# Two results to x's staging buffer and four more C slots in a matmul of undone prefix sums

## The chip, the cores and the metric

The kernel runs on 1 core of one Trainium2 chip. The metric is the device time of one execution in microseconds; lower is better. Before the change the median of three runs is 1509.22 us (1507.74 to 1509.64).

## The reference

```python
B, S, D = 8, 2048, 2048          # x: [8, 2048, 2048] float32, w: [2048, 2048] float32
cs = np.cumsum(x, axis=1)
diff = cs - (cs moved down by one row, zeros first)   # which is x again
return np.matmul(diff, w)        # float32
```

The difference of neighbouring prefix sums is x, so the kernel computes x @ w: a matrix of 16384 x 2048 by one of 2048 x 2048.

## The kernel before, in words

The rows of x are cut into 128 row tiles of 128 rows (`P = 128`, `END = 128`). The kernel has three parts.

**Plain part (row tiles 0 to 3, `PLAIN = 4`).** While w arrives, these tiles are multiplied as bf16. The sums stand in the eight banks of TensorE's accumulator memory, first for the left half of the columns (h = 0), then for the right (h = 1). `plain_out` copies finished banks of 128 x 512 to buffers on ScalarE (ACT) and notes them in `done`, and `put` stores them later: the first round from GpSimd's queue, the second, with one left-over product of tile 3, from SyncE's (SP). The buffers are two halves of `F[:, 2]` for tile 0 in the first round; a `wb` buffer of the pool `ring` for tile 0 in the second; and a buffer `o` of the pool `opool`, which has five, for all others. In the first round five results take an `o`. In the second it is six, and `left_over` takes a seventh. A buffer that is asked for again is free when its last store has landed.

`F` has five places of 128 x 1024 f32 in which the halves of later tiles of x are staged; `where` says which: tiles 4 and 6 use `F[:, 0]`, `F[:, 3]` and `F[:, 1]`, `F[:, 4]`, tile 7 `F[:, 2]` and `F[:, 3]`, tile 5 part of `xP`, in which the four plain tiles stood.

**First group of four row tiles (`group_plain`, tiles 4 to 7).** The rest is done in f16 with a seven-product (Strassen-like) scheme over 2 x 2 blocks. x is loaded (`load`), weighed for its scale (`weigh` on ACT, `scale_of` on VectorE, DVE), narrowed to f16 in place (`narrow`, ACT) and transposed by DMA from SP (`turn`). In the group `g` is tile 4, `h` tile 6, `g + 1` tile 5, `h + 1` tile 7. `product` (line 516) multiplies into a pair of banks called X, Y, Z or V; `keeps` (line 543, ACT) copies a pair of banks, scaled, to a pair of C slots; `adds` (line 546, DVE) adds a pair of banks to it; `puts` (line 557, SP) stores the pair and gives the slots back. `total` (line 506, DVE) makes sums of blocks of x such as S1, `block` (lines 357 and 361) narrows w's blocks, and `less` (line 499, DVE) makes differences of them. All x DMAs and the stores share SP's queue, in program order.

The order of the keeps in `group_plain` is C11g, C11h, C22 (of g + 1), C12g, C12h, C22 (of h + 1), C21 (g + 1), C21 (h + 1). Each takes two slots from the front of the list `free`; `put` appends a slot at the end when its store is issued in the program.

**Later groups (`group`, tiles 8 to 127, 30 groups).** The same scheme with one more level for some of the products (`quarter`, line 535).

What sets the order: each engine's instructions are chained in program order by `after`; the framework places tiles in memory, and makes the first user of a tile wait until the last users of whatever stood in that memory are done. The pools of the plain part (`ring`, `o`, `first` with `xP`) are closed before `C` and `inner` are opened, so these lie where those lay: the 7 slots of C where the ring's buffers lay, `inner` (24 pieces of 128 x 512 f16) where the `o` buffers and most of `xP` lay. `inner` holds sums of x (pieces 0 to 7) and differences of w (pieces 8 to 23; pieces 16 to 23 are written by `in_3.first()`, near the end of `group_plain`).

Of the kernel before, what the change touches and what calls it, by code (L numbers as in the profile page):

```python
# [10 lines left out]
def kernel(  # L11
# [18 lines left out]
    f32 = mybir.dt.float32  # L30
# [11 lines left out]
    PLAIN = 4  # L42
# [33 lines left out]
    def after(engine, ask):  # L76
        if engine in last:
            with tc.issue_after(last[engine].ins):
                said = ask()
        else:  # L80
            said = ask()
        last[engine] = said[-1] if isinstance(said, tuple) else said
        return said
# [77 lines left out]
    with tc.tile_pool(name="ring", bufs=7) as ring, tc.tile_pool(  # L161
# [81 lines left out]
        def here(h, r):  # L243
            return range(1 if h == 0 and r == PLAIN - 1 else 2)
# [14 lines left out]
        def put(c, rows, columns, queue=nc.gpsimd):  # L259
            return queue.dma_start(out2[rows, columns], c)  # L260

        def plain_out(h, r):
            for n in here(h, r):
                if h == r == 0:
                    c = F[:, 2, ds(n * NB, NB)]
                elif h == 0 or r > 0:
                    c = opool.tile([P, NB], f32, name="o")
                else:
                    c = ring.tile([P, NH], bf16, name="wb").bitcast(f32)
                after("act", lambda: nc.scalar.copy(c, ps[r][n]))  # L270
                done.append((c, ds(r * P, P), ds(h * NH + n * NB, NB)))
# [22 lines left out]
        for ko in range(KO - KQ):  # L294
# [9 lines left out]
            if ko in turns:  # L304
                q, a = turns[ko]
# [15 lines left out]
        for r in range(PLAIN):  # L321
            for ko in range(KO - KQ, KO):
                plain(0, r, ko)
            plain_out(0, r)
# [22 lines left out]
        with tc.issue_after(whole_max.ins):  # L347
            for c, rows, columns in done:
                put(c, rows, columns)
# [15 lines left out]
        def finish_row(r):  # L365
            for ko in range(KO - KQ, KO):
                plain(1, r, ko)
            plain_out(1, r)
# [45 lines left out]
        for c, rows, columns in done:  # L414
            after("sp", lambda: put(c, rows, columns, nc.sync))
# [34 lines left out]
    inner = inpool.tile([P, 24, NB], f16, name="inner")  # L450
# [6 lines left out]
    S1 = [Part(inner[:, ds(2 * i, 2), :]) for i in range(2)]  # L457
    passing = [Quarter(inner[:, j, :]) for j in range(4, 8)]
    free = [cpool.tile([P, NB], f32, name=f"c{i}") for i in range(7)]

    def pair():
        return [one_c() for _ in range(2)]
# [92 lines left out]

    def put(c, t, at):
        after("sp", lambda: nc.sync.dma_start(out2[ds(t * P, P), ds(at * NB, NB)], c))
        free.append(c)

    store = put  # L560

    def puts(c, t, h):
        for n in range(2):
            put(c[n], t, 2 * h + n)
# [446 lines left out]
```

## Time and profile before

| | |
|---|---|
| Time, median of 3 runs (lowest, highest) | 1509.22 us (1507.74, 1509.64) |
| Span of the profiled execution, first to last instruction | 1507.4 us |
| Its own time beside the span | not shown on the page |
| DVE, ACT busy | 88%, 61% of the span |
| DMA traffic | 354 MB, 235 GB/s mean |
| Plain part, `group_plain`, later groups on TensorE | about 0 to 76, 76 to 134, 134 to 1507 us |

The profile names engines PE (TensorE's matmuls), PEld (its weight loads), DVE, ACT, POOL (GpSimd) and SP. A row of a timeline has start, duration, engine, line, operation, output and inputs, and how many equal instructions were merged; in brackets stands the idle time of the engine before it and what ended it. A row of the waits has the total in us, how often, and the longest. A row of DMA issues has the queue, the count, the KB of each and the median us from issue to landing.

### The profile page before, as it was taken

Reading aid. Unit: us, or ns where it says so; the run is one execution under the profiler, and the core shown is the slowest. Engines: PE = TensorE matmul, PEld = TensorE weight load, DVE = VectorE, ACT = ScalarE, POOL = GpSimd, SP = SyncE. Lnnn points to the kernel's source line nnn. Section 1 sums busy time; section 2 is a strip of 40 time slices with the busy share of each in tenths; the row PEclk is TensorE's granted clock in tenths of the full one; section 3 lists DMA queues with packets and bytes.
Section 4 is the critical chain, followed back from the end, with each engine's and each line's share of the span. In section 5 each row is a group of like instructions: output and inputs, shape, how many; then the busy total and the mean of one; then the engine's idle time right before and its main releaser. Section 6 shows DMA issues by size and latency. Waiting matters only on the chain.

```text
span 1507.4 us, 21215 instructions
## 1 busy us (share of the span) xinstructions
PE 1480.5 (98%) x6799; PEld 661.8 (44%) x6799; DVE 1329.6 (88%) x2419; ACT 914.2 (61%) x1301; POOL 328.9 (22%) x360
## 2 busy tenths in 40 slices
PE   8988999999999999999999999999999999999998
PEld 3433444444444444444444444444444444444443
DVE  7987778889998899998899998999898899888997
ACT  5865656656656656656656656556656556666552
POOL 0100001122221122222122222122222122212222
PEclk9999999999999999999999999999999999999999
DMA  9988979988888988788987888987788988888962
GB/s 359 354 216 243 248 228 249 254 243 211 232 223 229 253 242 212 235 221 233 252 244 205 235 220 240 249 245 205 233 217 244 256 224 219 233 219 241 253 177 105
DMA packets 378912, 354.28 MB, mean 235 GB/s; under 512 B 274928, under 2 KB 275440, under 8 KB 378672
## 3 DMA queue, kind: packets, MB, share of 16 engines
q1 hardware_dynamic: 378240, 351.09, 83.5%
q0 software_dynamic: 560, 1.84, 0.3%
q8 instruction: 53, 0.87, 0.2%
q14 instruction: 59, 0.48, 0.1%
HBM read 151.52 MB, written 136.31 MB: 191 GB/s over the span
## 4 chain that ended last, share of the span: by engine, by line
PE 75%; DVE 13%; issue 4%; DMA 4%; ACT 3%; SPq 0%; DVEq 0%; ACTq 0%
PE b L535 37%; PE b L516 36%; DVE c L546 9%; DVE inner L506 3%; DMA W<-in_w_dram 2%; PE b L250 2%; ACT c L543 1%; DMA x<-F 1%; DVE W L499 1%; DMA W<-in_x_dram 0%; DMA out_dram<-c 0%; DVE x L506 0%; ACT W L361 0%; ACT waste L112 0%; DVE m L129 0%
## 5 line engine op out<-in xcount | busy, mean ns | idle before, releaser
L546 DVE SCALAR_TENSOR_TENSOR c<-b,u,c 128x512 f32<-128x512 f32 x1048 | 736.6, 745 | 125.4 <-PE b L535 81.3
L516 PE MATMUL b<-W,x 128*128 128x512 f16 x3072 | 717.9, 380 | 5.9 <-ACT c L543 3.8
L543 ACT ACTIVATE c<-b,u 128x512 f32<-128x512 f32 x496 | 315.5, 680 | 283.6 <-issue 147.8
L516 PEld LDWEIGHTS <-x 128*128 128x128 f16 x3072 | 300.9, 98 | 370.5 <-issue 8.4
L143 ACT ACTIVATE F<-F,s 128x1024 f16<-128x1024 f32 x246 | 282.4, 1148 | 162.3 <-DVE s L131 158.3
L535 PE MATMUL b<-W,inner 128*128 128x512 f16 x1392 | 338.3, 379 | 0.0
L112 ACT ACTIVATE waste<-F 128x1024 uint8<-128x1024 f32 x246 | 259.5, 1055 | 115.0 <-DMA F<-in_x_dram 110.9
L535 PEld LDWEIGHTS <-inner 128*128 128x128 f16 x1744 | 168.5, 98 | 215.3 <-DVE c L546 15.3
L132 POOL TENSOR_SCALAR u<-m,uw 128x1 f32<-128x1 f32 x124 | 66.6, 542 | 817.0 <-DVE m L129 809.0
L535 PEld LDWEIGHTS <-x 128*128 128x128 f16 x1560 | 152.1, 98 | 195.9 <-issue 14.6
L535 PE MATMUL b<-W,x 128*128 128x512 f16 x968 | 234.2, 379 | 1.5
L503 POOL TENSOR_TENSOR flow<-W 128x512 f16<-128x512 f16 x140 | 163.6, 1195 | 291.2 <-PE b L535 286.8
L506 DVE TENSOR_TENSOR x<-x,x 128x1024 f16<-128x1024 f16 (+1 forms) x214 | 147.2, 700 | 6.2 <-PE b L516 1.1
L503 POOL TENSOR_TENSOR flow<-W,W 128x512 f16<-128x512 f16 x84 | 94.9, 1160 | 0.0
L535 PE MATMUL b<-flow,x 128*128 128x512 f16 x352 | 90.3, 379 | 2.5 <-DVE c L546 2.5
L506 DVE TENSOR_TENSOR inner<-x,x 128x1024 f16<-128x1024 f16 (+1 forms) x122 | 67.4, 553 | 3.3 <-DMA x<-F 3.3
L250 PE MATMUL b<-wb,xP 128*128 128x512 bf16 x240 | 57.4, 393 | 5.0 <-ACT wb L234 3.6
L535 PE MATMUL b<-inner,x 128*128 128x512 f16 x240 | 61.6, 379 | 0.7 <-DVE x L506 0.7
L535 PE MATMUL b<-inner 128*128 128x512 f16 x240 | 61.6, 379 | 0.4 <-DVE c L546 0.4
L506 DVE TENSOR_TENSOR inner<-x,inner 128x512 f16<-128x512 f16 x60 | 51.7, 862 | 0.0
L112 ACT ACTIVATION_READ_ACCUMULATOR waste<-F 128x1 f32 x246 | 46.6, 190 | 0.0
L506 DVE TENSOR_TENSOR x<-inner,x 128x1024 f16<-128x1024 f16 x62 | 42.4, 683 | 3.2
(56 smaller groups left out, 510.2 us busy)
## 6 DMA issues: line engine op xcount, KB each, us to landing
out_dram<-c SPq DMA_DIRECT2D x496, 256.0 KB, 3.2
F<-in_x_dram SPq DMA_DIRECT2D x246, 512.0 KB, 4.9
W<-in_w_dram SPq DMA_DIRECT2D x32, 512.0 KB, 9.6
W<-in_x_dram SPq DMA_DIRECT2D x16, 256.0 KB, 7.7
x<-F SPq DMA_TRANSPOSE x246, 3.4
out_dram<-o SPq DMA_DIRECT2D x7, 256.0 KB, 3.6
spill<-flow SPq DMA_DIRECT2D x3, 512.0 KB, 2.6
out_dram<-o POOLq DMA_DIRECT2D x5, 256.0 KB, 4.2
```

The lines of the kernel that those rows point to most:

```text
L112: lambda: nc.scalar.activation(waste, where[t][i], ABS, scale=1.0 / ROW, accum_out=sums_of[t][:, i : i + 1],),
L132: after("pool", lambda: nc.gpsimd.tensor_scalar(u, m, uw, None, MUL))
L143: lambda: nc.scalar.activation(narrowed(t)[:, ds(i * NH, NH)], where[t][i], COPY, scale=s),
L250: lambda: nc.tensor.matmul(ps[r][n], xP[:, r, ko, :], wb[h, ko][:, ds(n * NB, NB)], start=(ko == 0), stop=(ko == KO - 1),),
L499: after("dve", lambda: nc.vector.tensor_tensor(dst[k], p[k], q[k], SUB))
L503: after("pool", lambda: nc.gpsimd.tensor_tensor(passed[k], i.t21[k], i.Q2[k], SUB))
L506: after("dve", lambda: nc.vector.tensor_tensor(dst.all, p.all, q.all, op))
L516: said = nc.tensor.matmul(to[n], a[k], b[k][:, n, :], start=(first and k == 0), stop=(k == KH - 1), skip_group_check=True,)
L535: said = nc.tensor.matmul(to, a[k], b[k], start=(first and k == 0), stop=(k == 3), skip_group_check=True)
L543: after("act", lambda: nc.scalar.activation(c, p, COPY, scale=u))
L546: after("dve", lambda: nc.vector.scalar_tensor_tensor(c, p, u, c, MUL, ADD))
```

## The change

In the second round the two results of plain row tile 3 go to the halves of `F[:, 2]`, as those of tile 0 do in the first round. Four more slots for C, called `extra`, are cut out of `inner`: pieces 16 and 17, 18 and 19, 20 and 21, 22 and 23, each read as 128 x 512 f32. They stand at the front of `free`, so the first four keeps take them, and `put` doesn't give them back. All engines issue the same operations in the same order as before; only buffers and waits differ.

```diff
         def plain_out(h, r):
             for n in here(h, r):
-                if h == r == 0:
+                if (h, r) in ((0, 0), (1, PLAIN - 1)):
                     c = F[:, 2, ds(n * NB, NB)]
                 elif h == 0 or r > 0:
                     c = opool.tile([P, NB], f32, name="o")
...
     free = [cpool.tile([P, NB], f32, name=f"c{i}") for i in range(7)]
+    extra = [inner[:, ds(j, 2), :].rearrange("p a c -> p (a c)").bitcast(f32) for j in range(16, 24, 2)]
+    free = extra + free
...
     def put(c, t, at):
         after("sp", lambda: nc.sync.dma_start(out2[ds(t * P, P), ds(at * NB, NB)], c))
-        free.append(c)
+        if not any(c is e for e in extra):
+            free.append(c)
```

## The prediction, made before the changed kernel ran

> **What bounds the kernel now.** I read the page's head first, then who waited for whom, then TensorE's timeline at the waits that the change touches, and last the queues behind these waits.
>
> ```profile
> span 1507.4 us, 21215 instructions
> PE 1480.5 (98%) x6799; PEld 661.8 (44%) x6799; DVE 1329.6 (88%) x2419; ACT 914.2 (61%) x1301; POOL 328.9 (22%) x360
> ```
>
> PE is the bound: 1480.5 of 1507.4 us. An edit pays only where it removes idle time of PE, and only if nothing takes it back before the steady groups begin. The waits on stores, and PE's own waits, are these:
>
> ```profile
> ACT c L543 <- DMA out_dram<-c: 8.7, 3, 5.8
> ACT o L270 <- DMA out_dram<-o: 5.8, 1, 5.8
> PE b L516 <- ACT c L543: 3.8, 2, 3.4
> PE b L516 <- DVE inner L506: 2.3, 1, 2.3
> PE b L516 <- ACT o L270: 1.7, 1, 1.7
> ```
>
> ACT waits once for 5.8 us until an o buffer is stored, and once for 5.8 us until a C buffer is. PE's timeline (start, duration, what, idle before it) has the price of both:
>
> ```profile
> 75.70 4.05 PE L516 MATMUL b<-W,x 128*128 128x512 f16 x18
> 81.41 10.09 PE L516 MATMUL b<-W,x 128*128 128x512 f16 x46 [1.66 <-ACT o L270]
> 93.77 3.61 PE L516 MATMUL b<-W,inner 128*128 128x512 f16 x16 [2.27 <-DVE inner L506]
> ...
> 101.29 10.67 PE L516 MATMUL b<-W,x 128*128 128x512 f16 x48 [0.44 <-ACT c L543]
> ...
> 115.25 0.38 PE L516 MATMUL b<-W,x 128*128 128x512 f16 x1
> 119.01 11.34 PE L516 MATMUL b<-W,x 128*128 128x512 f16 x44 [3.38 <-ACT c L543]
> ```
>
> Together 1.66 + 2.27 + 0.44 + 3.38 = 7.75 us. The last gap costs more than itself, as two windows show (us, PE busy and count, granted clock, DMA share, GB/s):
>
> ```profile
> 92.00:96.00 4.00, 2.23 (x11) 1.00 0.90 260
> 119.01:124.00 4.99, 4.99 (x16) 0.66 0.50 197
> ```
>
> A full PE starts a matmul every 0.216 us: the row at 81.41 has 46 in 10.09 us, of which the last takes 0.38, so (10.09 - 0.38) / 45. In the 4.99 us after the 3.38 us gap 23 would fit; the granted clock is 0.66 and there are 16, so 7 x 0.216 = 1.5 us more. After the 2.27 us gap the clock stayed at 1.00. What the edits can touch is thus 7.75 + 1.5 = 9.3 us, 0.6% of the span.
>
> **Part 1: two results of row tile 3 go to F.** Their copies were the sixth and seventh users (with the left-over product's) of five o buffers; now only five are asked for in that round. No instruction is added: two copies and two stores keep their places and sizes and change their buffer. ACT's queue around them:
>
> ```profile
> 73.45 1.54 ACT L270 COPY o<-b 128x512 f32<-128x512 f32 x3
> 80.78 0.59 ACT L270 COPY o<-b 128x512 f32<-128x512 f32 x1 [5.78 <-DMA out_dram<-o]
> 81.97 0.69 ACT L384 ACTIVATE o<-b,uw 128x512 f32<-128x512 f32 x1 [0.61 <-DMA out_dram<-o]
> ...
> 85.36 2.33 ACT L143 ACTIVATE xP<-xP,s 128x1024 f16<-128x1024 f32 x2 [0.48 <-DVE s L131]
> 87.60 3.21 ACT L361 ACTIVATE W<-W,uinv 128x1024 f16<-128x1024 f32 x3
> 90.72 1.24 ACT L543 ACTIVATE c<-b,u 128x512 f32<-128x512 f32 x2
> ```
>
> The fourth copy would start at 74.9 and end at 75.5; the left-over product is done when PE turns to the next line at 75.70, so its copy runs at 75.95, 6.0 us earlier than 81.97. Behind it tile 5 is weighed and narrowed. Is its data there? SP's timeline has the load's issue, the view of DMAs its size and time to landing, DVE's timeline the work ahead of the scale:
>
> ```profile
> 68.99 0.33 SPq L404 DMA_DIRECT2D xP<-in_x_dram  x1
> xP<-in_x_dram SPq DMA_DIRECT2D x1, 1024.0 KB, 5.3
> 70.72 8.02 DVE L357 TENSOR_SCALAR W<-W,uinv 128x1024 f16<-128x1024 f32 x12
> ```
>
> It landed at 68.99 + 5.3 = 74.3. From the left-over copy to the narrowing it takes 85.36 - 81.97 = 3.4 us, the last 0.5 of them for DVE's scale, and DVE is free of its blocks at 78.74. So narrowing tile 5 moves by the full 6.0 us, from 85.36 to 79.35, and B22's three blocks end at 84.8 instead of 90.8. PE's gap of 1.66 goes: bank 7 is free at 75.5.
>
> The cost of F: tile 7's first load goes to the same part of F and now waits for those two stores. They are issued on SP at about 79.8 and 80.3 and land some 4 us later (rows below), so at 84.3; SP reaches that load after tile 5's transposes, at 83.9. Cost 0.4 us on a load that starts 4.8 us earlier than before: nothing, as ACT weighs tile 7 only after the B22 blocks.
>
> **Part 2: four more C slots.** C11g and C11h, the first four results, take them, are never put back, and the seven old slots begin with C22g. No instruction moves. What changes is who waits for which store. Going through the list by hand: before, C12h[1] took the slot of C11h[0], whose store is the first of the six at 111.80; now C12h takes slots that were never used. C22h[1] took a slot long free; now it takes that of C12g[0], whose store is the third of the same six. So the wait doesn't vanish, it moves one step down and to a store 1.2 us later:
>
> ```profile
> 111.78 0.69 ACT L543 ACTIVATE c<-b,u 128x512 f32<-128x512 f32 x1 [3.47 <-PE b L516]
> 118.27 0.69 ACT L543 ACTIVATE c<-b,u 128x512 f32<-128x512 f32 x1 [5.80 <-DMA out_dram<-c]
> ...
> 122.22 2.32 ACT L143 ACTIVATE F<-F,s 128x1024 f16<-128x1024 f32 x2
> ```
>
> SP's timeline has that store's issue, and the view of DMAs its KB and us to landing:
>
> ```profile
> 112.95 0.47 SPq L557 DMA_DIRECT2D out_dram<-c  x1
> out_dram<-c SPq DMA_DIRECT2D x1, 256.0 KB, 6.5
> ```
>
> The third store lands at 112.95 + 6.5 = 119.45 by the old clock of events. ACT can then keep C22h[1] until 120.15 and go on to narrow tile 10, which stood at 122.22: 2.05 us saved on ACT. On PE, the product into Y starts at 115.25 at once and ends 16 x 0.216 = 3.45 us later, at 118.7; the next product's second matmul needs Z's second bank, free at 120.2. A gap of 1.3 us takes the place of the 3.5 us from matmul to matmul (119.01 - 115.25, less one spacing) and of 1.5 us of slow clock: PE saves 3.7 us, if the clock holds as it did after 2.27.
>
> **The wait that part 2 adds.** The extra slots lie in the tile named inner, which was first written by DVE's sum S1. Now ACT writes it first, with C11g[0], and so it is ACT that waits until that memory's last users are done: the o stores, and both transposes that read tile 5 out of xP (the changed program lists these semaphores at that instruction). Behind it in ACT's queue stand three B22 blocks, tile 7's weighing, and all later keeps. When does this wait end? In SP's timeline and the view of DMAs (KB, us to landing) stand the last o stores, one of them alone, and the two transposes, the second alone:
>
> ```profile
> 76.18 6.84 SPq L260 DMA_DIRECT2D out_dram<-o  x7
> 79.82 0.47 SPq L260 DMA_DIRECT2D out_dram<-o  x1
> out_dram<-o SPq DMA_DIRECT2D x1, 256.0 KB, 3.9
> 86.53 2.62 SPq L156 DMA_TRANSPOSE x<-xP  x2
> 87.87 1.29 SPq L156 DMA_TRANSPOSE x<-xP  x1
> x<-xP SPq DMA_TRANSPOSE x1, 3.3
> ```
>
> The store at 79.82 is the fifth of the seven; two more at its pace of 0.5 us free SP at 81.3 (before, they waited for ACT until 83.0). The transposes follow: the second starts at 81.3 + 1.34 = 82.65 and lands 3.3 later, at 85.95, if the engines are free; behind stores that land until about 85 it may be 87.1. I take 86.3, nearer the bare row. ACT is ready at 84.8, so it waits 1.5 us, and C11g's keep moves from 90.72 to 86.4: of the 6.0 us, 4.3 are left. Below: 85.0 (no wait, gain 5.7). Above: 87.1 (gain 3.6). The old S1 waited for the same transposes on DVE, at no cost.
>
> **The sum.** Up to 101 us: PE's work without gaps from 75.70 would reach the S1 product (93.77) after 18 + 46 matmuls, at 89.5; S1 follows C11g's keep and releases PE 4.3 us earlier, at 89.5 too. So 4.2 us is saved there. ACT, now 4.3 earlier, leaves most of the gap at 101.29. PE at 115: 4.3 earlier. Part 2: PE another 3.7 (8.0 in all), but ACT, and with it DVE's scales, its adds and SP's queue, only another 2.05, so 6.4 in all. What is late next is where these meet, in the timelines of DVE, PE and SP and in a window (busy time and count of PE, PEld, DVE, ACT and POOL, clock, DMA share, GB/s):
>
> ```profile
> 149.31 0.69 DVE L506 TENSOR_TENSOR inner<-x,x 128x1024 f16<-128x1024 f16 x1 [1.11 <-DMA x<-F]
> 152.35 1.02 PE L535 MATMUL b<-flow,x 128*128 128x512 f16 x4 [1.78 <-DVE c L546]
> 159.21 1.04 PE L535 MATMUL b<-inner,x 128*128 128x512 f16 x4 [0.66 <-DVE x L506]
> 140.46 6.83 SPq L156 DMA_TRANSPOSE x<-F  x2
> 132.00:166.00 34.00, 31.07 (x142) 13.46 (x141) 25.47 (x58) 21.61 (x33) 2.17 (x3) 1.00 1.05 249
> ```
>
> In the next group DVE's S1h waits for tile 11's transposes, PE for an add behind it. These transposes stand on SP behind stores of C22h and C12h, so they come 6.4 earlier, not 8.0. PE, up to 1.6 us ahead of them, waits up to 3.4 us instead of 1.78, and from 152 on all is 6.4 us earlier. Later groups have nearly no idle PE and no wait that the change touches. So the span becomes 1507.4 - 6.4 = 1501.0. The page shows no time but the span; the median of the runs is 1509.2, 1.8 above it, and I carry that over: 1502.8.
>
> [...]
>
> **Rivals.**
> *Half clock at the new gap.* The gap of up to 3.4 us at 152 lies between 2.27 (no drop) and 3.38 (drop). If the clock falls, PE loses 1.5 us again, of which the 0.66 us gap at 159.21, set by DVE and ACT, hides about half: 1502.8 + 0.9 = 1503.7. [...] Chance 0.2.
> *The store and the transposes come sooner.* With ACT's wait at 84.8 gone and the third store no later than PE, all 9.3 us are saved, if tile 11 also keeps up: 1499.9. For it: the wait has only 1.5 us to lose. Against: six stores land late as a block. Chance 0.13.
> *Tile 11's transposes do not move as much.* Two of them held SP for 6.83 us at 140.46, against 2.62 at 86.53: 4.2 us of queue, in a stretch with a DMA share of 1.05. If this hold grows by as much, because transfers now crowd into a full queue, 2.2 us are left: 1507.0. Against: the lull before it (a share of 0.50 from 119 to 124) takes in what comes earlier. Chance 0.12.
> *It doesn't do what it says.* If the new wait ends only where the old keep stood (90.7) and PE's slow stage is kept by the moved store wait, nothing is won: 1509. Chance 0.04.
> *Slower.* The slots go round in another order for the 30 later groups. If one keep in each waited for its store, the gain is gone at 6.4 / 30 = 0.21 us a group, and at 0.35 us the time is 1502.8 + 10.5 = 1513.3. Against: the first row of the waits has three such waits in the whole run, and seven slots still go round first in, first out. Chance 0.04.
>
> **How the numbers follow.** The forecast has 0.47. Range: from the second rival's 1499.9 to the third's 1507.0; this leaves out the last two and the edges. A measurement of this kernel can tell 0.2%, 3.0 us: faster is below 1506.2. That holds the forecast, the first two rivals and a quarter of the third: 0.83; three quarters of the third and most of the fourth are the same: 0.12; the last and the rest are slower: 0.05.
>
> **What would show it.** Right: no ACT wait on a store at the copies to o or F; C11g's keep near 86.4 after a wait for the transposes x<-xP of about 1.5 us; PE without gaps from 75.7 to about 96; a wait on a store at C22h[1] instead of C12h[1], PE's gap there about 1.3 us and the clock at 1.00; S1h in the next group near 142.9. Wrong: tile 5's transposes landing after 88, PE's gap at C22h over 2.5 us, S1h later than 146, or waits of c on stores that recur in every group.

## The result, and the profile after

The changed kernel takes 1502.92 us (median of 5 runs, 1500.95 to 1503.45) against 1508.17 us for the kernel before (5 runs, 1507.74 to 1509.64). The ratio is 0.9961, 95% interval 0.9949 to 0.9974: 3.9 to 7.7 us faster, 5.3 by the medians. In a second comparison it took 1502.34 us, ratio 0.996 (0.9946 to 0.9973). The profiled execution has a span of 1500.3 us, 7.1 less than the one before (of the runs of before, the profiled one is among the longer, of the changed kernel among the shorter).

The waits after (total us, times, longest), those that answer to the rows shown of before:

```profile
ACT c L545 <- DMA out_dram<-c: 6.3, 4, 2.5
ACT inner L545 <- DMA x<-xP: 3.2, 1, 3.2
PE b L518 <- DMA F<-in_x_dram: 1.4, 1, 1.4
PE b L518 <- ACT c L545: 0.8, 3, 0.4
```

No copy to an o buffer or to F waits for a store any more. The wait on a C store is 2.5 us at its longest instead of 5.8, and a wait of 3.2 us for the transposes that read xP is new. PE's timeline:

```profile
75.51 13.98 PE L518 MATMUL b<-W,x 128*128 128x512 f16 x64
90.85 3.61 PE L518 MATMUL b<-W,inner 128*128 128x512 f16 x16 [1.36 <-DMA F<-in_x_dram]
94.30 3.63 PE L518 MATMUL b<-W,x 128*128 128x512 f16 x16
98.38 0.38 PE L518 MATMUL b<-W,x 128*128 128x512 f16 x1 [0.44 <-ACT c L545]
98.95 10.30 PE L518 MATMUL b<-W,x 128*128 128x512 f16 x47 [0.20 <-ACT c L545]
...
116.57 17.21 PE L518 MATMUL b<-W,x 128*128 128x512 f16 x79 [0.19 <-ACT c L545]
...
145.12 1.02 PE L537 MATMUL b<-flow,x 128*128 128x512 f16 x4 [1.88 <-DVE c L548]
```

The 64 matmuls from 75.51 now run in one piece. The gap ahead of the S1 product shrank from 2.27 to 1.36 us (the view names a load; what came last is S1 on DVE, in the next block, which ends at 90.50: PE starts 0.35 us behind it). The gap of 3.38 us is 0.19. ACT, DVE and SP at the same places:

```profile
75.71 0.69 ACT L384 ACTIVATE o<-b,uw 128x512 f32<-128x512 f32 x1 [0.42 <-PE b L375]
79.10 2.33 ACT L143 ACTIVATE xP<-xP,s 128x1024 f16<-128x1024 f32 x2 [0.48 <-DVE s L131]
81.34 3.22 ACT L361 ACTIVATE W<-W,uinv 128x1024 f16<-128x1024 f32 x3
87.78 1.26 ACT L545 ACTIVATE inner<-b,u 128x512 f32<-128x512 f32 x2 [3.22 <-DMA x<-xP]
...
115.83 0.69 ACT L545 ACTIVATE c<-b,u 128x512 f32<-128x512 f32 x1 [2.55 <-DMA out_dram<-c]
116.41 2.32 ACT L143 ACTIVATE F<-F,s 128x1024 f16<-128x1024 f32 x2
89.82 0.68 DVE L508 TENSOR_TENSOR inner<-x,x 128x1024 f16<-128x1024 f16 x1
142.08 0.69 DVE L508 TENSOR_TENSOR inner<-x,x 128x1024 f16<-128x1024 f16 x1 [1.20 <-DMA x<-F]
82.10 2.94 SPq L156 DMA_TRANSPOSE x<-xP  x2
...
133.80 2.06 SPq L559 DMA_DIRECT2D out_dram<-c  x2
135.96 4.14 SPq L156 DMA_TRANSPOSE x<-F  x2
```

And the clock, in the windows behind the two gaps (us, PE busy and count, granted clock, DMA share, GB/s):

```profile
116.57:120.00 3.43, 3.43 (x16) 1.00 0.39 142
145.12:149.00 3.88, 3.88 (x18) 1.00 0.95 297
```

### The profile page after: what moved, and what is told of

Read it like the earlier page. It is cut to its first block, busy times and chain, and to the rows that moved or that the text cites. A ratio compares the mean times of both kernels' runs of the same rounds, so it can differ in the third digit from the quotient of the medians.

```text
span 1500.3 us, 21209 instructions
## 1 busy us (share of the span) xinstructions
PE 1477.7 (98%) x6793; PEld 660.9 (44%) x6799; DVE 1329.1 (89%) x2419; ACT 914.2 (61%) x1301; POOL 329.0 (22%) x360
## 4 chain that ended last, share of the span: by engine, by line
PE 74%; DVE 13%; issue 4%; DMA 4%; ACT 3%; SPq 0%; DVEq 0%; ACTq 0%
PE b L537 37%; PE b L518 35%; DVE c L548 9%; DVE inner L508 3%; PE b L250 2%; DMA W<-in_w_dram 2%; ACT c L545 2%; DMA F<-in_x_dram 1%; DVE W L501 1%; DMA x<-F 1%; DVE x L508 0%; DMA W<-in_x_dram 0%; DMA out_dram<-c 0%; ACT waste L112 0%; DVE m L129 0%
```

## The experiments

Four questions were open: which part carries the gain, what the new wait at C11g costs, what the wait at C22h[1] costs, and what decides when tile 11's transposes land. My theory: ACT's chain carries all of it, and hands it on through tile 11's transposes on SP to S1h. The rivals: the moved store wait and the clock carry it; or the full DMA queue decides, whatever ACT does. The start of X's first product differs by up to 1.4 us between profiles (74.77 to 76.16), so the table counts from it (75.70 before, 75.51 after). C11g's keep stands for its first half, [1] for the second half of a pair.

| kernel | C11g's keep | C12h[1] | C22h[1] | S1h | time, us | ratio to before (interval) |
|---|---|---|---|---|---|---|
| before | 15.0 | 42.6 | 45.9 | 73.6 | 1508.2 to 1509.0 | 1 |
| changed | 12.3 | 34.2 | 40.3 | 66.6 | 1502.9 | 0.9961 (0.9949 to 0.9974) |
| changed, again | 12.0 | 33.9 | 41.0 | 67.7 | 1502.3 | 0.9960 (0.9946 to 0.9973) |
| part 1 alone | 8.9 | 37.7 | 41.1 | 67.3 | 1503.9 | 0.9969 (0.9959 to 0.9980) |
| part 2 alone | 15.2 | 37.8 | 44.7 | 71.3 | 1507.0 | 0.9989 (0.9980 to 0.9998) |
| slots over the ring | 8.9 | 31.7 | 38.3 | 64.9 | 1501.2 | 0.9953 (0.9940 to 0.9965) |
| six slots | 11.5 | 33.4 | 36.9 | 65.3 | 1501.5 | 0.9956 (0.9943 to 0.9968) |
| six, and over the ring | 8.9 | 31.7 | 35.2 | 64.1 | 1500.4 | 0.9945 (0.9932 to 0.9957) |
| the same, late stores | 8.9 | 31.7 | 35.2 | 63.1 | 1498.7 | 0.9935 (0.9923 to 0.9948) |
| sixth store | 11.0 | 32.9 | 42.0 | 68.9 | 1504.7 | 0.9976 (0.9966 to 0.9986) |

Down the table the time follows S1h. Part 2 alone brings it 2.3 us earlier and takes 2.1 us less than the kernel before beside it, part 1 alone 6.3 and 5.1, slots over the ring 8.7 and 7.9, late stores 10.5 and 10.0. The intervals of most of the kernels below overlap, so a difference between two of their medians alone shows little.

### Part 1 alone

```diff
-    free = extra + free
+    extra = []
```

> Part 1 alone: row tile 3's two results go to F, C keeps its seven slots. Theory (ACT's chain carries the gain, and part 1 gives it at the start): the copies end by 75.5, tile 5 is narrowed at 79.1, C11g's keep runs at 84.6 without a wait, since it is not in the tile inner; PE has no gap before 89.4 and little at 98. From there all is 5.0 us earlier than before, the wait for a store at C12h[1] stays (5 to 6 us on ACT, 3.3 us on PE) and so may the slow clock after it; S1h of the next group at 144.3 instead of 149.3. Time 5 us under before: 1503.2. Rival (part 2's slots and the clock do most of it): at most 1.5 us under before, 1506.7, with S1h at 148.

1503.93 us. As the theory has it: no wait at C11g's keep, the wait of 6 us at C12h[1] in its old place, S1h at 143.46 (144.3 was said). ACT, then PE:

```profile
85.10 1.24 ACT L544 ACTIVATE c<-b,u 128x512 f32<-128x512 f32 x2
113.90 0.69 ACT L544 ACTIVATE c<-b,u 128x512 f32<-128x512 f32 x1 [5.98 <-DMA out_dram<-c]
114.63 20.66 PE L517 MATMUL b<-W,x 128*128 128x512 f16 x95 [3.56 <-ACT c L544]
114.63:118.00 3.37, 3.37 (x16) 1.00 0.53 210
```

Part 1 alone gives most of the change's gain, though PE still idles 3.56 us at the store; so the moved store wait and the clock do not carry it. What part 2 adds to it in the changed kernel is not shown: the intervals of the ratios overlap, and S1h (67.3) lies between the two profiles of the changed kernel (66.6 and 67.7). The last row was not expected: after a longer gap than before's 3.38 us, the clock stays at 1.00.

### Part 2 alone

```diff
-                if (h, r) in ((0, 0), (1, PLAIN - 1)):
+                if h == r == 0:
```

> Part 2 alone: four extra slots, row tile 3's results in o buffers as before. Theory: the wait at the o copy stays, tile 5 is narrowed at 85.4, its second transpose lands at 91.1, C11g's keep runs at 91.2 (0.4 us later than before), PE keeps its gaps of 1.7 and 2.3 us. Then C12h does not wait, C22h[1] waits for the third store (119.5), PE's gap of 3.4 us falls to 1.3 with the clock at 1.00, and ACT is 2.0 us earlier, so that S1h comes at 147.5. Time 1.7 us under before: 1506.5. Rival (PE's own saving of 3.7 us comes through): 1504.5. Rival (the new wait costs as much as the old one): no change, 1508.2.

1506.95 us, a gain of 0.3 to 3.0 us; 1506.5 was expected. The o copy waits 5.42 us, C11g's keep comes 0.2 us later than before, and from there ACT is 1.2 us earlier at C22h[1] and S1h 2.3 us. SP comes 1.2 us earlier to the two stores ahead of tile 11's transposes, and these stores and transposes hold it for 6.6 us instead of 7.8 (137.97 to 144.61; 139.47 to 147.29 before). PE's own saving, 3.0 us where the next group's first `quarter` starts (137.92 against 141.20, each counted from its own start), does not come through in full. The clock fell here at another place, after the gap ahead of the S1 product, which takes back some of PE's saving too (the 16 matmuls take 5.30 us, 3.61 in the kernel before):

```profile
93.69 5.30 PE L518 MATMUL b<-W,inner 128*128 128x512 f16 x16 [2.88 <-DMA F<-in_x_dram]
94.20:97.50 3.30, 3.30 (x10) 0.50 0.92 307
```

### The extra slots over the ring's memory

```diff
+    tails = ctx.enter_context(tc.tile_pool(name="tails", bufs=1))
     cpool = ctx.enter_context(tc.tile_pool(name="C", bufs=1))
...
-    inner = inpool.tile([P, 24, NB], f16, name="inner")
+    tail = tails.tile([P, 8, NB], f16, name="tail")
+    inner = inpool.tile([P, 16, NB], f16, name="inner")
...
-    spare = [inner[:, j, :] for j in range(8, 24)]
+    spare = [inner[:, j, :] for j in range(8, 16)] + [tail[:, j, :] for j in range(8)]
...
-    extra = [inner[:, ds(j, 2), :].rearrange("p a c -> p (a c)").bitcast(f32) for j in range(16, 24, 2)]
+    extra = [tail[:, ds(j, 2), :].rearrange("p a c -> p (a c)").bitcast(f32) for j in range(0, 8, 2)]
```

> The changed kernel with the extra slots (and in_3's differences) in a tile of their own that lies where the ring's buffers lay, not where xP lay; same memory in all. Theory (the wait of 3.2 us at C11g's keep is the placement's, and is worth time): that wait is gone, the keep runs at 84.6 instead of 87.8; S1 is then bound by tile 5's transposes, at 87.5, PE has no gap at 89.4 and none at 98, so PE at the Y product of C12h is 2.0 us earlier (107.1 instead of 109.1). S1h at 140 instead of 142.1, time 2.0 us under the changed kernel's: 1500.9. Rival (the transposes of tile 11 wait in a full DMA queue and do not come earlier): S1h stays at 142, time 1502.9.

1501.15 us. The keep runs without a wait, 3.3 us earlier than in the changed kernel, and PE has no gap before 106 us. S1h gains 1.7 us against the first profile of the changed kernel; that the time is less as well is likely, but the intervals overlap:

```profile
84.82 1.23 ACT L547 ACTIVATE tail<-b,u 128x512 f32<-128x512 f32 x2
114.19 0.69 ACT L547 ACTIVATE c<-b,u 128x512 f32<-128x512 f32 x1 [3.06 <-DMA out_dram<-c]
140.76 0.69 DVE L510 TENSOR_TENSOR inner<-x,x 128x1024 f16<-128x1024 f16 x1 [1.53 <-DMA x<-F]
```

So the new wait belongs to where the slots lie, not to there being more of them: four slots over memory whose last users were done do not have it.

### Six extra slots

```diff
-    extra = [inner[:, ds(j, 2), :].rearrange("p a c -> p (a c)").bitcast(f32) for j in range(16, 24, 2)]
+    extra = [inner[:, ds(j, 2), :].rearrange("p a c -> p (a c)").bitcast(f32) for j in range(12, 24, 2)]
```

> The changed kernel with six extra slots, pieces 12 to 23 of inner: C11g, C11h and C22g take them, and no keep of this group takes a slot whose store is under way. Theory (C22h[1]'s wait for the third store, 2.55 us on ACT, sets when tile 10 is narrowed, and this sets SP's queue up to tile 11's transposes): that keep runs at 113.2 instead of 115.8, tile 10 is narrowed at 113.8, S1h comes at 139.5 to 140 instead of 142.1, PE's gap of 1.88 us there is gone; time 2.0 us under the changed kernel's: 1500.9. Rival (full DMA queue): the keep is earlier, but S1h stays within 0.7 us of 142.1, time 1502.7. C11g's wait of 3.2 us stays in both.

1501.46 us. C22h[1] no longer waits. Tile 10 is narrowed at 114.01 instead of 116.41. SP reaches the two stores ahead of tile 11's transposes at 131.24 instead of 133.80, 2.4 us earlier counted from the start, and the transposes at 132.25 instead of 135.96; but these hold it for 6.38 us instead of 4.14, and S1h gains 1.2 us:

```profile
114.01 2.33 ACT L143 ACTIVATE F<-F,s 128x1024 f16<-128x1024 f32 x2 [1.04 <-DVE s L131]
131.24 0.90 SPq L559 DMA_DIRECT2D out_dram<-c  x2
132.25 6.38 SPq L156 DMA_TRANSPOSE x<-F  x2
140.72 0.69 DVE L508 TENSOR_TENSOR inner<-x,x 128x1024 f16<-128x1024 f16 x1 [1.33 <-DMA x<-F]
143.77 1.02 PE L537 MATMUL b<-flow,x 128*128 128x512 f16 x4 [2.01 <-DVE c L548]
145.00:148.30 3.30, 3.30 (x10) 0.50 1.02 342
```

Both were right in part: without the wait S1h comes earlier (whether the time is less can't be told, the intervals overlap), and of the 2.4 us that SP has gained ahead of those stores about half is gone at S1h. The DMA share is 1.05 from 124 to 128 us and 1.02 from 145.00 to 148.30, ahead of this stretch and behind it, so a full queue would fit this; it is not shown apart from other causes here. My expectation that PE's gap there goes away was wrong: it is 2.01 us, since PE gained too, and the clock halved after it.

### The changed kernel, again

> The changed kernel once more, beside the next three on one chip. Both theories: 1502 to 1503.5, S1h of the next group near 142, C22h[1] waiting 2 to 3 us for the third store, C11g's keep some 3 us for tile 5's transposes. The granted clock may fall or not at the gap of 1.9 us at 145.

1502.34 us. The wait at C11g is 3.01 us and the one at C22h[1] 3.42, above the 2 to 3 expected; S1h is at 142.50. This profile has the slow clock after PE's gap of 2.42 us at 145, which the first one has not:

```profile
145.54 1.86 PE L537 MATMUL b<-flow,x 128*128 128x512 f16 x4 [2.42 <-DVE c L548]
145.54:148.70 3.16, 3.16 (x8) 0.50 0.94 310
```

### Six extra slots, over the ring

The last two edits together: C11g and C22g take slots over the ring, C11h two in inner (pieces 12 to 15).

> Both repairs together: six extra slots, of which C11g and C22g take those over the ring's memory and C11h two in inner. Neither C11g's keep nor C22h[1] waits (84.6 and about 110). Theory now (each repair alone moved its keep by 2.5 to 3 us, but tile 11's transposes landed only 1.3 us earlier, because they stand in a full DMA queue): together they land near 140 too, S1h at 140.2, time 1500.9, no better than one repair. Rival (the two gains add): S1h at 139.4 or earlier, time 1499.8.

1500.44 us, between the two. Beside the kernel with slots over the ring alone, C22h[1] is kept 3.1 us earlier and S1h comes 0.8 us earlier; SP holds tile 11's transposes for 6.79 us. So the gains neither add nor vanish, and whether the time differs from one repair's can't be told (the intervals overlap). PE's gap here is 2.51 us, and the clock stays at 1.00 behind it:

```profile
142.85 1.02 PE L540 MATMUL b<-flow,x 128*128 128x512 f16 x4 [2.51 <-DVE c L551]
142.85:146.20 3.35, 3.35 (x16) 1.00 0.96 308
```

### Late stores

```diff
         keeps(C21, Y, vh)
-        puts(C21, h + 1, 0)
...
         turn(h + 5)
+        puts(C21, h + 1, 0)
```

on top of the kernel just above.

> The kernel with both repairs, and C21h's two stores are issued after tile 11's transposes instead of before them. Theory (what stands ahead of these transposes in the DMA queue sets S1h): two stores of some 0.65 us each less ahead, S1h 1.3 us earlier than in the kernel with both repairs, PE's gap there 1.3 us smaller, time 1.2 us less. Rival (the transposes are late for another reason, ACT's narrowing or SP's issue): S1h within 0.4 us of the kernel with both repairs, same time.

1498.72 us, the best of all: 1.7 us less than without this edit, and 3.6 less than the changed kernel beside it. The intervals overlap, but all five runs lie below four of the five without this edit. ACT's keeps stand where they stood, and so does its narrowing of tile 11 (52.4 us after the start in both); S1h comes 1.0 us earlier, with PE's gap 1.53 us:

```profile
137.98 0.69 DVE L511 TENSOR_TENSOR inner<-x,x 128x1024 f16<-128x1024 f16 x1 [0.86 <-DMA x<-F]
141.03 1.02 PE L540 MATMUL b<-flow,x 128*128 128x512 f16 x4 [1.53 <-DVE c L551]
```

So the two stores ahead of these transposes cost S1h 1.0 us, and ACT does not set it by then. Without them SP also reaches the transposes 1.1 us earlier, so whether their issue on SP or their bytes in the queue cost it is not told apart.

### The sixth store

```diff
-        C22 = pair()
+        C22 = [free.pop(0), free.pop()]
         keeps(C22, Z, vh)
```

in the changed kernel.

> The changed kernel, but C22h[1] takes the slot whose store is the sixth of the six instead of the third. Theory (this keep waits for its store to land): its store lands at 117.5 instead of 115.7, the keep runs 1.8 us later, PE's gap ahead of its second bank grows from 0.2 to 2.0 us. Of the 1.8 us, 0.5 to 1.8 reach S1h (142.6 to 143.9), as the DMA queue hides a part; time 0.5 to 1.8 us over the changed kernel's: 1503.4 to 1504.7. Rival (this wait costs nothing, the DMA queue hides it all): same time, S1h at 142.

1504.73 us (8 runs, 1503.42 to 1507.33), 2.4 us over the changed kernel beside it (5 runs, 1501.52 to 1503.82); 0.5 to 1.8 was expected. C22h[1] waits 5.54 us, S1h comes 1.2 us later than in that kernel by the table, and the gap of PE is larger than expected:

```profile
117.40 0.69 ACT L545 ACTIVATE c<-b,u 128x512 f32<-128x512 f32 x1 [5.54 <-DMA out_dram<-c]
118.14 17.21 PE L518 MATMUL b<-W,x 128*128 128x512 f16 x79 [3.18 <-ACT c L545]
147.34 1.86 PE L537 MATMUL b<-flow,x 128*128 128x512 f16 x4 [2.54 <-DVE c L548]
118.14:121.50 3.36, 3.36 (x16) 1.00 0.04 7
147.34:150.60 3.26, 3.26 (x8) 0.50 0.95 322
```

The store wait costs time, and which store it is decides how much. Within this one profile a gap of 3.18 us left the clock at 1.00 and one of 2.54 us halved it.

## Why the prediction was right

The time forecast was 1502.8 us and 1502.92 was measured. The forecast started from the median of three runs, 1509.2; with five it is 1508.2. So the measured gain by medians is 5.3 us, not 6.4; 6.4 lies in the interval. The mechanism was mostly right, but that the two times agree to 0.1 us is luck: the start was 1.0 us too high, the wait at C11g 1.7 us longer than forecast, and the steps behind it gave more than forecast. Step by step:

- **Part 1.** Right. The left-over copy at 75.71 (75.95), tile 5's narrowing at 79.10 (79.35), nothing waits for F's stores. Alone this part gives 1503.93. In detail, row tile 3's copies were the fifth and sixth users of the o buffers and the left-over product's the seventh.
- **The added wait.** Right in kind, mis-sized. ACT waited 3.22 us at C11g's keep, not 1.5, and the keep ran at 87.78, outside the bounds given for it (85.0 to 87.1). SP came to the transposes at 82.10 instead of 81.3, and the second landed at 87.4, 3.9 us after its start, where the row of before had 3.3: in the 4 us ahead of them the DMA share was 0.13 before (84 to 88 us) and 1.06 now (80 to 84). So by 101 us PE had saved 2.9 us (2.7 counted from the start), not 4.3, and kept a gap of 1.36 us.
- **Part 2.** Right in kind: C12h does not wait, C22h[1] waits for the third store. ACT waited 2.55 us there and PE's gap was 0.19 us instead of 1.3, mostly because PE itself came 1.6 us later than forecast (112.55 against 115.25 - 4.3), so that less of the store's time was left to wait for. The clock stayed at 1.00. The account of what stood there before was wrong: C22h[1] had not "a slot long free". By the list, C12h took c1 and c2 and C22h c3 and c6, and c6 was C12g[0]'s, so this keep waited for the third store before as well. That store had landed at 119.5 when the keep ran at 121.65, since the wait at C12h[1] had held ACT longer. So the wait at C22h[1] is not new: taking away the one ahead of it laid it open.
- **The meeting at tile 11.** Right: PE's lead is lost there. S1h came at 142.08 (142.9), PE's gap was 1.88 us (up to 3.4). The transposes held SP for 4.14 us instead of 6.83, though the two stores just ahead of them held it for 2.06 instead of 0.90; together that is 6.3 us instead of 7.8. The forecast let this hold stand, so this step gave 1.5 us more than forecast: at C22h[1] the kernel was 0.7 us behind the forecast (115.83 against 119.45 - 4.3), at S1h 0.8 us ahead of it. What made the hold shorter is not shown.
- **The rivals.** The half clock did not come in the first profile of the changed kernel and came in the second; its price was right to the order (0.5 us where 0.9 was said: from the row behind the gap to the first row of 32 matmuls of 128x512 it took 13.94 us with the halving, 13.43 without), the condition (between 2.27 and 3.38 us of gap) was wrong. The 0.2 given to it was the author's estimate. The "sooner" rival needed what two further edits did: with both waits away the kernel takes 1500.4, where 1499.9 was said. The third, that the queue at tile 11 takes the gain back, was borne out in kind by six slots, but at this gain it hid nothing: stores and transposes held SP for less, not more. The slower rival did not occur: waits of C on stores are four in the whole run, 2.5 us at the longest.

## What to carry to other kernels

Before slots are added, list by hand, for the kernel before and for the one after, which store each later user of a slot waits for: one wait can hide the next. Here four slots more took away the wait for the first store of six, and the one for the third, which had been there all along, still cost 2.5 us of ACT; two slots more ended both waits. Memory lent from a tile that is opened later brought that tile's first-use wait along (3.2 us on ACT), to another engine and an earlier time; as many slots over memory that is long free ran without the wait of 3.2 us, and the next group's S1h came 1.7 us earlier. Follow a gain to where the engines meet again: of 2.4 us that SP gained ahead of two stores and two transposes, 1.2 us reached the sum that waits for them.

## What the runs showed of the hardware that was not expected

The length of an idle gap of PE did not decide alone whether its clock halved. Halved (granted clock 0.50 in windows of 3.16 to 3.39 us behind the gap): after gaps of 2.01 (six slots), 2.42 (changed, again), 2.54 (sixth store), 2.88 (part 2 alone) and 3.38 us (before). Not halved (1.00 in windows of 3.35 to 3.88 us behind the gap): after 1.88 (changed), 2.27 (before), 2.51 (six, and over the ring), 3.18 (sixth store) and 3.56 us (part 1 alone). Nor after 2.18 (part 2 alone) and 2.20 us (slots over the ring), by the row of 20 matmuls behind the gap: it takes 4.48 us there, as behind the gap of 1.88 us, and 5.25 to 6.17 us behind those of 2.01, 2.42 and 2.54 us.

In the kernel before, the clock was still 1.00 in the first 0.66 us behind the gap of 3.38 us (119.01 to 119.67) and 0.50 from 119.69 to 123.08, with 10 matmuls, where the next 3.40 us have 17. By the clock records of its trace the half clock lasted 3.41 us, between stretches of full clock of 102.40 and 1382.40 us, which are 30 and 405 times 3.413 us; the changed kernel's first profile has one of 1484.80 us, 435 times as long. So in these two traces the limits of the clock's stretches lie whole multiples of 3.41 us apart, and where a gap lies between them may count. That is the author's reading, worked out afterwards, with no run made for it: what decides whether the clock halves is not shown.
